# Start order, tails by column half and a norm by columns in a one-core decoder kernel

## The chip, the cores and the metric

The kernel runs on one core of one Trainium2 chip. The metric is the device time of one execution in microseconds, from launch to end, with inputs and outputs in the chip's memory. A core has five engines with queues of their own: TensorE (PE in the profile, with its weight loads PEld), VectorE (DVE), ScalarE (ACT), GpSimd (POOL) and SyncE (SP, which here issues nearly all DMAs). [...]

## The reference, cut to what matters

Input x has 256 positions of 2048 float32 features. Two layers follow each other; every layer is a mixer and then a gated ConvFFN, and both add to x.

```python
def gla_mixer(x, ...):                      # layer 0
    xn = rms_norm(x, norm_w)
    q, k, v, g = split(xn @ w_in)           # 1024, 1024, 2048, 2048 columns
    log_a = log_sigmoid((xn @ gk_w1) @ gk_w2 + gk_b) / 16
    ...                                     # chunked linear attention, 4 heads
    return (rms_norm(o) * silu(g)) @ w_out

def moba_mixer(x, ...):                     # layer 1; 256 positions are one block
    q = rms_norm(rms_norm(x, norm_w) @ w_q) # per head
    k, v = split(rms_norm(x, kv_norm) @ kv_w)
    ...                                     # causal softmax with a relative bias
    return o @ w_out

def conv_ffn(x, norm_w, w_up, conv_w, conv_b, w_down):
    h = rms_norm(x, norm_w) @ w_up          # 2048 -> 2 * 5632
    a, u = split(causal depthwise conv of width 3 over h, plus conv_b)
    return (silu(a) * u) @ w_down           # 5632 -> 2048
```

An rms_norm divides each position by the root of the mean square over its 2048 features and multiplies by a gain for each feature. The kernel multiplies the gain into x before the matrix product and divides by the root only after it.

## The kernel before, in words

Weights are streamed once. `WeightStream` reads them in chunks of 128 x 2048 float32 (1 MB) into three buffers `wraw`, on SP's queue, and hands them out as halves of 1024 columns. A half is split for TensorE into a rounded part `whi` (ACT, line 120) and a remainder `wlo` (DVE, line 121); every product is formed from hi x hi, hi x lo and lo x hi. Three pairs of `whi`/`wlo` buffers rotate, so splitting runs up to two halves ahead of TensorE (`AHEAD`). Fetching a half is a `step()`. Before it fetches, `step()` runs the jobs that are due: `after(n, job)` registers a job for n steps later. That is how norms, transposes and attention are placed between matrix products. The final order of the instructions on each engine is set by the scheduler of the framework when the program is built, from its own estimate of times; dependencies are kept for whole tiles.

The residual lives transposed, feature by position: eight tiles `h[p]` of 256 features x 256 positions, loaded by SP in `load_x` (line 190) between the first weight chunks (`ws.cuts`, `ws.lead`, lines 192 to 205). `make_xw` (lines 213 to 220) forms the gained operand `xw` of one pair p: hi on ACT (line 217), remainder on DVE (line 218). `add_squares` (222) accumulates squares, `token_rstd` (249) sums them over features: `spread_sum` (242) with two matmuls against a matrix of ones gives the root for all 256 positions along the free axis, and with `columns` two more matmuls (line 254) give it as two columns, one position to a partition; `rsqrt` (230) turns the sums into 1/root with Ln and Exp on ACT and one Newton step.

The order of the work:

- Values (`w_v`): `gemm_tok` (289), four groups of 512 columns, each over the eight pairs of x, one step of 12 matmuls a pair; the result has positions on partitions, and `v_out` (356) scales it by the column form of the root.
- Keys, queries, gate and output projection: `gemm` (275).
- FFN up: 44 times `gemm`, two steps each. FFN down: `down` (597), two blocks of 1024 output columns. A block goes over 22 pairs k of hidden features in the order of `ORDERS`; a pair marked "+" is done in seven products of 128 x 128 x 512 in place of eight (Strassen's scheme, which needs sums of weights, lines 94 to 96, on DVE), a plain pair in eight. The eight accumulators are PSUM banks p[1] to p[8]; p[2] and p[3] are the two halves of one tile `low`, p[4] and p[8] tiles of their own. p[2] and p[4] take the first 512 columns (for the two halves of the positions), p[3] and p[8] the other 512. After a block's last seven-product pair `u_sums` (659) combines the Strassen banks; after its last step `sums` adds the four others (line 726 in layer 0, line 705 in layer 1).
- In layer 0 the two blocks come out position by feature and are turned back by `back` (730): four transposes (line 737), an add into `h[q]` (739), then `nrm.feed(q)`, which makes the operand for the next product. The first four run inside block 1, the last four after the following product `w_mq` has begun; `after(5, nrm.close)` ends the norm. `h` has been parked in DRAM meanwhile and is loaded back by POOL (`load_back`).
- In layer 1 the sums are written to the output, 256 KB a time, three by SP and one by ACT (line 707).
- `bias_rows` (775) prepares the relative bias; `head_norm` (794) needs the column form of `n_q`; nothing reads its other form.

Of the kernel before, what the change touches and what calls it, by code (L numbers as in the profile page):

```python
# [8 lines left out]
F32 = mybir.dt.float32  # L9
# [28 lines left out]
def _order(text):  # L38
# [6 lines left out]
           _order("0 2 4 6 8 10 1+ 12 3+ 14 5+ 16 7+ 17 9+ 18 11+ 19 13+ 20 15+ 21")],  # L45
          [_order("0 2 4 1+ 6 3+ 8 5+ 10 7+ 12 16 9+ 14 11+ 17 13+ 18 15+ 19 20 21"),
           _order("0 1+ 2 3+ 4 5+ 6 7+ 8 16 9+ 10 11+ 12 17 13+ 14 15+ 18 19 20 21")]]


class WeightStream:  # L50
# [4 lines left out]
    def __init__(self, nc, raw, parts):  # L55
        self.nc, self.raw, self.parts = nc, raw, parts
# [4 lines left out]
        self.sums, self.slot = {}, None  # L61
# [37 lines left out]
    def prefetch(self, i):  # L99
        nc = self.nc  # L100
        while self.n_split < len(self.halves):
            n = self.n_split
            c, o, kind = self.halves[n]
            if n > i + self.AHEAD + (kind != "plain"):
                break
            self._dma(c + 1)
            for c_, _, kind_ in self.halves[n:n + 3]:
                if kind_ == "b11" and c_ not in self.sums:
                    self._dma(c_ + 1)
                    self._sums(c_)  # L110
            src = self.sums[c][kind] if kind in ("t13", "t24") else self.tiles[c][:, o:o + 1024]
            if kind == "b11":
                src = src[:, :512]
            if kind != "plain" and n % 4 == 3:
                hi, lo = self.slot([128, 1024], F32R, "whi"), self.slot([128, 1024], F32R, "wlo")
            else:
                hi = self.parts.tile([128, 1024], F32R, name="whi")
                lo = self.parts.tile([128, 1024], F32R, name="wlo")
            for a, b in ((0, 512), (512, 1024)) if n == 0 else ((0, src.shape[1]),):
                nc.scalar.copy(hi[:, a:b], src[:, a:b])  # L120
                nc.vector.tensor_sub(lo[:, a:b], src[:, a:b], hi[:, a:b].bitcast(F32))  # L121
# [15 lines left out]
def trunk(ctx: ExitStack, tc: tile.TileContext, xT, cst, msk, w1p, w2a, w_k, w_qa, w_v, w_g, w_go,  # L137
# [23 lines left out]
    ws = WeightStream(nc, raw, parts)  # L161
    plan = [(w_v, 4, 8192), (w_k, 4, 4096), (w_qa, 4, 4096), (w_g, 8, 4096), (w_go, 8, 4096),
# [42 lines left out]
    ws.lead[5, 0] = [load_rest]  # L205
# [4 lines left out]
    def col(c):  # L210
        return cs[:, c:c + 1]

    def make_xw(p, c, name):
        x = slot([128, 2, 2 * S], F32R, name)
        for i in range(2):
            n = col(c + 2 * p + i)
            A.activation(x[:, i, :S], h[p][:, i, :], AF.Copy, scale=n)  # L217
# [4 lines left out]
    def add_squares(p, acc):  # L222
        if p == 0:
            A.activation(acc, h[p], AF.Square)
        else:
            sq = temp("hsq")
            A.activation(sq, h[p], AF.Square)
            V.tensor_add(acc, acc, sq)
# [20 lines left out]
    def token_rstd(acc, columns):  # L249
# [39 lines left out]
    def gemm_tok(xs):  # L289
        ps = acc_ps.tile([128, 2, 512], F32, name="acc")  # L290
        for q0 in range(0, KT, 2):
            hi, lo = step()
            for k in range(2):
                kt = q0 + k
                x = xs(kt)
                wh, wl = hi[:, k * 512:(k + 1) * 512], lo[:, k * 512:(k + 1) * 512]
                for t in range(2):
                    xh, xl = x[:, 128 * t:128 * t + 128], x[:, S + 128 * t:S + 128 * t + 128]
                    T.matmul(ps[:, t, :], xh, wh, start=kt == 0, stop=False)  # L299
                    T.matmul(ps[:, t, :], xh, wl, start=False, stop=False)  # L300
                    T.matmul(ps[:, t, :], xl, wh, start=False, stop=kt == KT - 1)  # L301
        ws.prefetch(cur[0])
        return ps
# [21 lines left out]
    class Norm:  # L325


        def __init__(self, c, name, columns=False):
            self.c, self.name, self.columns, self.xs = c, name, columns, []
# [27 lines left out]
    def v_out(v, ps, n):  # L357

        r0, r1 = (n.rstd[:, S + t:S + t + 1] for t in range(2))
# [237 lines left out]
    def down(layer, hid, ready, jobs):  # L597
# [5 lines left out]
        for b, order in enumerate(ORDERS[layer]):  # L603
# [31 lines left out]
            for i, (k, seven) in enumerate(order):  # L635
# [20 lines left out]
            ws.prefetch(cur[0])  # L656
            sums(b, p)

    def u_sums(p, r):
# [33 lines left out]
    def last_down(hid):  # L693
        def ready(b, p):
# [8 lines left out]
            def end(b, p):  # L703
                for x, n, t, c in zip(r, (2, 3, 4, 8), (0, 0, 1, 1), (0, 1, 0, 1)):
# [13 lines left out]
    def first_down(hid, nrm):  # L718
        blocks = {}

        def ready(b, p):
            blocks[b] = r = u_sums(p, None)

            def end(b, p):
                for x, n in zip(r, (2, 3, 4, 8)):
                    V.tensor_add(x, x, p[n])
# [41 lines left out]
    n_q = Norm(C_MN, "xw", True)  # L768
# [25 lines left out]
    def head_norm(ps, name):  # L794
        t_, sq = slot([128, 2, 512], F32, name), slot([128, 2, 512], F32, "hsq")
        for t in range(2):
            r = n_q.rstd[:, S + t:S + t + 1]
# [73 lines left out]
    after(1, bias_rows)  # L871
# [57 lines left out]

def _quads(w, orders):  # L930
# [4 lines left out]
    q = np.stack([q[g][:, [k for k, _ in order]] for g, order in enumerate(orders)])  # L935
    return _chunks(q.reshape(n // 1024, 128, -1))
# [71 lines left out]
```

## Time and profile before

| | |
|---|---|
| median of 3 runs | 2235.82 us (2235.37 to 2242.01) |
| profiled execution | 2235.57 us |
| its span, first to last instruction | 2233.8 us |
| PE busy | 2212.4 us, 11778 matmuls |
| DVE, ACT, POOL busy | 1659.1, 1263.9, 42.4 us |
| read from HBM | 420.22 MB |

A row of the timeline gives the start and the length in us, then the engine, the line of the kernel, the operation, what it writes and reads, and in brackets how long the engine had been idle and what released it. "x6" merges six like instructions. SPq, ACTq and POOLq are the queues in which DMAs are issued. In the list of waits the numbers are the total in us, the count and the longest. PE's matmuls overlap, so the spacing of their starts and not their length tells the rate.

### The profile page before, as it was taken

How to read it: one execution, taken by the hardware profiler on the slowest of the kernel's cores; microseconds unless marked ns; L12 is line 12 of the kernel's file. 1: busy time of each engine (PE TensorE's matmuls, PEld its weight loads, DVE VectorE, ACT ScalarE, POOL GpSimd, SP SyncE). 2: the span in 40 equal slices, each digit the busy share in tenths (PEclk: the TensorE clock that was granted, in tenths of full speed). 3: DMA queues.
4: the chain of work that ended last, by engine and by line, in shares of the span. 5: the costliest groups of instructions: out<-in, count | busy, mean ns of one | idle time of the engine just before them, and what ended most of it. 6: DMA issues, size and time to landing. Idle time of an engine off the chain costs nothing.

```text
span 2233.8 us, 30207 instructions
## 1 busy us (share of the span) xinstructions
PE 2212.4 (99%) x11778; PEld 1899.6 (85%) x11778; DVE 1659.1 (74%) x2283; ACT 1263.9 (57%) x1759; POOL 42.4 (2%) x59
## 2 busy tenths in 40 slices
PE   7999999999999999999999999999999999999999
PEld 6889888888888888788878888888888888888887
DVE  6566776787777777878866676567777777788886
ACT  6555654655555555545556565456555555555553
POOL 0000000000000000000010000000000000000000
PEclk9999999999999999999999999999999999999999
DMA  6554456555555555565655545456555555556653
GB/s 239 188 188 146 160 198 215 195 189 195 192 191 189 189 189 189 208 222 174 233 202 189 172 168 170 164 192 201 198 189 189 190 189 190 192 194 214 240 202 142
DMA packets 63441, 428.49 MB, mean 192 GB/s; under 512 B 7441, under 2 KB 7969, under 8 KB 13378
## 3 DMA queue, kind: packets, MB, share of 16 engines
q1 hardware_dynamic: 59634, 415.43, 54.1%
q0 software_dynamic: 3232, 10.56, 1.4%
q8 instruction: 92, 1.51, 0.3%
q10 hardware_dynamic: 432, 0.57, 0.1%
q14 instruction: 51, 0.42, 0.1%
HBM read 420.22 MB, written 6.32 MB: 191 GB/s over the span
## 4 chain that ended last, share of the span: by engine, by line
PE 94%; DVE 3%; DMA 2%; issue 1%; ACT 0%; SPq 0%; DVEq 0%; ACTq 0%
PE acc L284 39%; PE acc L285 20%; PE acc L624 10%; PE p L624 6%; PE acc L300 5%; PE acc L301 5%; PE acc L299 5%; DMA wraw<-w_dn 2%; DVE wlo L121 1%; DVE t L94 1%; PE sT L482 0%; ACT whi L120 0%; PE tr L814 0%; DMA wraw<-w_v 0%; PE s L832 0%
## 5 line engine op out<-in xcount | busy, mean ns | idle before, releaser
L121 DVE TENSOR_TENSOR wlo<-wraw,whi 128x1024 fp32r<-128x1024 f32 (+1 forms) x785 | 937.4, 1200 | 441.7 <-ACT whi L120 436.5
L120 ACT CAST whi<-wraw 128x1024 fp32r<-128x1024 f32 (+1 forms) x785 | 807.8, 1034 | 775.1 <-PE acc L284 448.9
L284 PE MATMUL acc<-xw,whi 128*128 128x512 f32 x3328 | 1157.9, 392 | 0.0
L285 PE MATMUL acc<-xw,wlo 128*128 128x256 f32 x3328 | 932.1, 280 | 0.0
L284 PEld LDWEIGHTS acc<-xw,whi 128*128 128x128 f32 x3328 | 622.8, 187 | 137.7
L285 PEld LDWEIGHTS acc<-xw,wlo 128*128 128x128 f32 x3328 | 628.7, 189 | 0.2
L624 PE MATMUL acc<-whi,hid 128*128 128x512 f32 x576 | 204.5, 390 | 0.0
L624 PE MATMUL p<-whi,hid 128*128 128x512 f32 x512 | 180.1, 390 | 0.0
L624 PEld LDWEIGHTS acc<-whi,hid 128*128 128x128 f32 x576 | 108.1, 188 | 22.5 <-ACT whi L120 0.4
L120 ACT CAST whi<-t 128x1024 fp32r<-128x1024 f32 x64 | 67.5, 1054 | 82.6 <-PE p L624 74.5
L624 PE MATMUL acc<-wlo,hid 128*128 128x512 f32 x288 | 112.8, 392 | 0.5 <-DVE wlo L121 0.3
L624 PEld LDWEIGHTS p<-whi,hid 128*128 128x128 f32 x512 | 96.1, 188 | 20.1
L299 PE MATMUL acc<-whi,xw 128*128 128x512 f32 x256 | 100.8, 394 | 12.4 <-ACT xw L217 11.6
L300 PE MATMUL acc<-wlo,xw 128*128 128x512 f32 x256 | 101.2, 395 | 1.0 <-DVE wlo L121 1.0
L301 PE MATMUL acc<-whi,xw 128*128 128x512 f32 x256 | 100.6, 393 | 0.0
L300 PE MATMUL acc<-wlo,xkv 128*128 128x512 f32 x256 | 100.6, 393 | 0.0
L299 PE MATMUL acc<-whi,xkv 128*128 128x512 f32 x256 | 100.5, 393 | 0.0
L301 PE MATMUL acc<-whi,xkv 128*128 128x512 f32 x256 | 100.4, 392 | 0.0
L581 ACT ACTIVATE au<-up,cs 128x256 f32<-128x256 f32 x176 | 95.9, 593 | 7.3 <-DVE up L577 7.3
L624 PE MATMUL p<-wlo,hid 128*128 128x512 f32 x256 | 99.7, 389 | 0.0
L121 DVE TENSOR_TENSOR wlo<-t,whi 128x1024 fp32r<-128x1024 f32 x64 | 77.8, 1221 | 25.8 <-ACT whi L120 25.4
L624 PE MATMUL acc<-whi,comb 128*128 128x512 f32 x256 | 89.9, 389 | 0.0
(254 smaller groups left out, 2356.6 us busy)
## 6 DMA issues: line engine op xcount, KB each, us to landing
wraw<-w_up SPq DMA_DIRECT2D x176, 1024.0 KB, 4.8
wraw<-w_dn SPq DMA_DIRECT2D x88, 1024.0 KB, 4.9
wraw<-w_g SPq DMA_DIRECT2D x16, 1024.0 KB, 4.8
wraw<-w_go SPq DMA_DIRECT2D x16, 1024.0 KB, 4.9
wraw<-w_mq SPq DMA_DIRECT2D x16, 1024.0 KB, 4.8
wraw<-w_kk SPq DMA_DIRECT2D x16, 1024.0 KB, 4.8
wraw<-w_kv SPq DMA_DIRECT2D x16, 1024.0 KB, 4.8
wraw<-w_mo SPq DMA_DIRECT2D x16, 1024.0 KB, 4.8
```

Source lines behind the costliest of these rows:

```text
L94: V.tensor_sub(t13, src[:, 512:1536], src[:, 0:1024])
L120: nc.scalar.copy(hi[:, a:b], src[:, a:b])
L121: nc.vector.tensor_sub(lo[:, a:b], src[:, a:b], hi[:, a:b].bitcast(F32))
L284: T.matmul(ps[:, b, :], hi[:, c:c + 128], x, start=kt == 0, stop=False)
L285: T.matmul(ps[:, b, :S], lo[:, c:c + 128], x[:, :S], start=False, stop=kt == kts - 1)
L299: T.matmul(ps[:, t, :], xh, wh, start=kt == 0, stop=False)
L300: T.matmul(ps[:, t, :], xh, wl, start=False, stop=False)
L301: T.matmul(ps[:, t, :], xl, wh, start=False, stop=kt == KT - 1)
L581: A.activation(au[:, i, :], t[:, i, :], AF.Identity, bias=col(cb + n), scale=col(cw + 2 * 2 * FT + n))
L624: T.matmul(p[n], xp, wp, start=n not in begun, stop=left[n] == 0)
```

## The change

Four things are done.

1. Start. The first two column groups of the values are stored side by side (`w_v2`) and computed together: `gemm_tok(xs, 2)` takes for each pair of x two steps, one for each group, in two accumulators. x is therefore needed half as often during the first 16 steps. Loads on SP are cut and ordered anew: 512 columns of weights, the two halves of x pair 0, 512 columns, 1024 columns, x pair 1, then whole chunks of 1 MB with one pair of x after each. The first norm's 16 gain columns get a tile of their own, `gn`, loaded first on ACT's queue, ahead of the rest of `cs` and of the activation table. `issue_after` puts the second half of the first weight split and the first squares behind the first operand on ACT.
2. Tails. Of each block of `down`, up to three plain pairs at the end (two in block 1 of layer 0, three in the others) are done first for the one half of the columns (p[2], p[4]) and then for the other (p[3], p[8]); `sums` runs once after each half. The weights are stored in that order. One entry of `ORDERS` changes, so that block 1 of layer 0 has two plain pairs at its end and five in place of six at its beginning.
3. After block 1 of layer 0. Turning back begins earlier: pairs 0 and 1 at index 2 of block 1, pair 4 inside its tail, pairs 5, 6 and 7 one, two and three steps into the next product; the norm closes after 4 steps. Parked tiles are loaded back at indices 0 and 1. `bias_rows` moves from 1 step to 12 steps into that product.
4. One norm by columns. `n_q` skips `spread_sum` and `rsqrt`; `column_rstd` makes two matmuls, a small DVE operation and a power on POOL.

The diff, without the plain consequences in names and arguments:

```diff
@@ -42,23 +42,28 @@
 ORDERS = [[_order("0 2 4 1+ 6 3+ 8 5+ 10 7+ 12 16 9+ 14 11+ 17 13+ 18 15+ 19 20 21"),
-           _order("0 2 4 6 8 10 1+ 12 3+ 14 5+ 16 7+ 17 9+ 18 11+ 19 13+ 20 15+ 21")],
+           _order("0 2 4 6 8 1+ 10 3+ 12 5+ 14 7+ 16 9+ 17 11+ 18 13+ 19 15+ 20 21")],
...
+def _tail(order):
+    return min(3, len(order) - 1 - max(i for i, (_, seven) in enumerate(order) if seven))
@@ -117,7 +122,8 @@
             for a, b in ((0, 512), (512, 1024)) if n == 0 else ((0, src.shape[1]),):
-                nc.scalar.copy(hi[:, a:b], src[:, a:b])
+                with self.tc.issue_after(self.first) if a else nullcontext():
+                    nc.scalar.copy(hi[:, a:b], src[:, a:b])
@@ -158,8 +164,8 @@
-    plan = [(w_v, 4, 8192), (w_k, 4, 4096), (w_qa, 4, 4096), (w_g, 8, 4096), (w_go, 8, 4096),
+    plan = [(w_v2, 1, 16384), (w_v, 2, 8192), (w_k, 4, 4096), (w_qa, 4, 4096), (w_g, 8, 4096), (w_go, 8, 4096),
@@ -181,17 +187,19 @@
     V.memset(one, 1.0)
+    gn = keep.tile([128, KT], F32, name="gn")
+    A.dma_start(gn, cst[:, C_GN:C_GN + KT])
+    A.dma_start(cs[:, :C_CW], cst[:, :C_CW])
...
     V.memset(mhalf, -0.5)
-    A.dma_start(cs[:, :C_CW], cst[:, :C_CW])
...
-    ws.cuts = {0: ((0, 512), (512, 1024), (1024, 1536), (1536, 2048)), 1: ((0, 1024), (1024, 2048))}
-    for p, at in ((0, (0, 0)), (1, (0, 512)), (2, (0, 1024)), (3, (1, 0)), (4, (1, 1024)), (5, (2, 0)), (6, (2, 0)),
-                  (7, (3, 0))):
+    ws.cuts = {0: ((0, 512), (512, 1024), (1024, 2048))}
+    for p, at in ((0, (0, 0)), (1, (0, 1024)), (2, (1, 0)), (3, (2, 0)), (4, (3, 0)), (5, (4, 0)), (6, (5, 0)),
+                  (7, (6, 0))):
@@ -202,26 +210,28 @@
-    ws.lead[5, 0] = [load_rest]
+    ws.lead[7, 0] = [load_rest]
...
     def col(c):
-        return cs[:, c:c + 1]
+        return gn[:, c - C_GN:c - C_GN + 1] if C_GN <= c < C_GN + KT else cs[:, c:c + 1]
...
             n = col(c + 2 * p + i)
-            A.activation(x[:, i, :S], h[p][:, i, :], AF.Copy, scale=n)
+            hi = A.activation(x[:, i, :S], h[p][:, i, :], AF.Copy, scale=n)
+            ws.first = ws.first or hi.ins
...
         if p == 0:
-            A.activation(acc, h[p], AF.Square)
+            with tc.issue_after(ws.first):
+                A.activation(acc, h[p], AF.Square)
@@ -250,11 +260,24 @@
         spread_sum(ps[:, :S], acc[:, 0])
-        for t in range(2 if columns else 0):
-            T.matmul(ps[:, S + t:S + t + 1], acc[:, 0, 128 * t:128 * t + 128], one, start=True, stop=True)
         n = S + 2 if columns else S
+        if columns:
+            sum_columns(ps[:, S:], acc)
...
         rsqrt(r[:, :n], ps[:, :n], 1.0 / D, (128, n))
+        return r[:, :S], r[:, S:]
+    def sum_columns(ps, acc):
+        for t in range(2):
+            T.matmul(ps[:, t:t + 1], acc[:, 0, 128 * t:128 * t + 128], one, start=True, stop=True)
+    def column_rstd(acc):
+        ps = bank("sum_h", (128, 2))
+        V.tensor_add(acc[:, 0], acc[:, 0], acc[:, 1])
+        sum_columns(ps, acc)
+        m, r = (small.tile([128, 2], F32, name=n) for n in ("mean_h", "col_h"))
+        V.tensor_scalar(m, ps, 1.0 / D, EPS, op0=OP.mult, op1=OP.add)
+        nc.gpsimd.tensor_tensor(r, m, mhalf[:, :2], op=OP.pow)
@@ -286,21 +309,22 @@
-    def gemm_tok(xs):
-        ps = acc_ps.tile([128, 2, 512], F32, name="acc")
+    def gemm_tok(xs, groups=1):
+        out_ = [acc_ps.tile([128, 2, 512], F32, name="acc") for _ in range(groups)]
         for q0 in range(0, KT, 2):
+            for ps in out_:
+                hi, lo = step()
+                for k in range(2):
+                    kt = q0 + k
...
         ws.prefetch(cur[0])
-        return ps
+        return out_ if groups > 1 else out_[0]
@@ -337,14 +361,17 @@
         def close(self):
-            self.rstd = token_rstd(self.acc, self.columns)
-    nrm = Norm(C_GN, "xw", True)
+            if self.rows:
+                self.rstd, self.col = token_rstd(self.acc, self.columns)
+            else:
+                self.col = column_rstd(self.acc)
+    nrm = Norm(C_GN, "xw", columns=True)
...
     for p in range(2, NP):
-        after(p - 1, lambda p=p: nrm.operand(p))
+        after(2 * p - 3, lambda p=p: nrm.operand(p))
@@ -428,9 +455,11 @@
     after(26, gate_decay)
-    for hd in range(GH):
+    for hd, ps in enumerate(gemm_tok(xs, 2)):
+        after(2 * hd + 1, lambda hd=hd, ps=ps: v_out(vg[hd], ps, nrm))
+    for hd in (2, 3):
         ps = gemm_tok(xs)
-        after((10, 3, 0, 0)[hd], lambda hd=hd, ps=ps: v_out(vg[hd], ps, nrm))
+        after(0, lambda hd=hd, ps=ps: v_out(vg[hd], ps, nrm))
@@ -632,7 +661,8 @@
             last = max(i for i, (k, seven) in enumerate(order) if seven)
-            for i, (k, seven) in enumerate(order):
+            tail = [k for k, _ in order[len(order) - _tail(order):]]
+            for i, (k, seven) in enumerate(order[:len(order) - len(tail)]):
@@ -653,8 +683,17 @@
                     sums = ready(b, p)
-            ws.prefetch(cur[0])
-            sums(b, p)
+            for f, (n0, n1) in enumerate(((2, 4), (3, 8))):
+                for i, k in enumerate(tail):
+                    for job in todo.get((f, i), ()):
+                        job()
+                    w = step()
+                    todo_ = [(n, t, a) for a in range(2) for n, t in ((n0, 0), (n1, 1))]
+                    for n, t, a in sorted(todo_, key=lambda x: x[1]) if i == len(tail) - 1 else todo_:
+                        prod(n, part(k, a, t), w, a)
+                if f:
+                    ws.prefetch(cur[0])
+                sums(f, (n0, n1))
@@ -672,11 +711,11 @@
         V.tensor_add(u3, u2, p[7])
+        V.tensor_add(r[2], r[2], u3)
         V.tensor_add(u2, u2, p[5])
+        V.tensor_add(u3, u3, p[5])
         V.tensor_add(r[1], r[1], u2)
-        V.tensor_add(r[2], r[2], u3)
         V.tensor_add(r[3], r[3], u3)
-        V.tensor_add(r[3], r[3], p[5])
@@ -700,8 +739,9 @@
-            def end(b, p):
-                for x, n, t, c in zip(r, (2, 3, 4, 8), (0, 0, 1, 1), (0, 1, 0, 1)):
+            def end(c, ns):
+                for t, n in enumerate(ns):
+                    x = r[2 * t + c]
@@ -753,19 +793,21 @@
-        jobs = {3 + q: [lambda q=q: back(q, in_acc)] for q in range(4)}
-        for m, i in enumerate((1, 2, 15, 16)):
+        jobs = {2: [lambda q=q: back(q, in_acc) for q in (0, 1)]}
+        for q, i in ((2, 3), (3, 4), (4, (1, 1))):
+            jobs.setdefault(i, []).append(lambda q=q: back(q, in_acc))
+        for m, i in enumerate((0, 1, 15, 16)):
...
         down(0, hid, ready, {1: jobs})
-        for q in range(4, NP):
-            after(1 + (q - 4) // 2, lambda q=q: back(q, lambda: bank("hf", (128, 2, S))))
-        after(5, nrm.close)
+        for q in (5, 6, 7):
+            after(q - 4, lambda q=q: back(q, lambda: bank("hf", (128, 2, S))))
+        after(4, nrm.close)
...
         after(6 + 2 * p, lambda p=p: park(p))
-    n_q = Norm(C_MN, "xw", True)
+    n_q = Norm(C_MN, "xw", rows=False, columns=True)
@@ -868,7 +910,7 @@
     xkv = []
-    after(1, bias_rows)
+    after(12, bias_rows)
```

`_both_groups` stores, for each 256 rows, the 1024 columns of group 0 and then those of group 1; `_quads` stores a block's tail by column halves.

More of the change, by code (lines that the diff above doesn't have):

```diff
@@ L1 @@
 import math
-from contextlib import ExitStack
+from contextlib import ExitStack, nullcontext
 import concourse.bass as bass
@@ L60, in __init__ @@
         self.cuts, self.lead = {}, {}
-        self.sums, self.slot = {}, None
+        self.sums, self.slot, self.first = {}, None, None
     def add(self, w, g, cols):
@@ L136, in trunk @@
 @with_exitstack
-def trunk(ctx: ExitStack, tc: tile.TileContext, xT, cst, msk, w1p, w2a, w_k, w_qa, w_v, w_g, w_go,
+def trunk(ctx: ExitStack, tc: tile.TileContext, xT, cst, msk, w1p, w2a, w_k, w_qa, w_v2, w_v, w_g, w_go,
           w_up0, w_dn0, w_kk, w_kv, w_mq, w_mo, w_up1, w_dn1, rel, onehot, out):
@@ L287, in gemm @@
         return ps
-    def gemm_tok(xs):
-        ps = acc_ps.tile([128, 2, 512], F32, name="acc")
+    def gemm_tok(xs, groups=1):
+        out_ = [acc_ps.tile([128, 2, 512], F32, name="acc") for _ in range(groups)]
         for q0 in range(0, KT, 2):
[L292 to L301, printed above, removed]
+            for ps in out_:
+                hi, lo = step()
+                for k in range(2):
+                    kt = q0 + k
+                    x = xs(kt)
+                    wh, wl = hi[:, k * 512:(k + 1) * 512], lo[:, k * 512:(k + 1) * 512]
+                    for t in range(2):
+                        xh, xl = x[:, 128 * t:128 * t + 128], x[:, S + 128 * t:S + 128 * t + 128]
+                        T.matmul(ps[:, t, :], xh, wh, start=kt == 0, stop=False)
+                        T.matmul(ps[:, t, :], xh, wl, start=False, stop=False)
+                        T.matmul(ps[:, t, :], xl, wh, start=False, stop=kt == KT - 1)
         ws.prefetch(cur[0])
-        return ps
+        return out_ if groups > 1 else out_[0]
     def rows(xs):
@@ L325, in trunk, with __init__ @@
     class Norm:
[L328 to L329 removed]
+        def __init__(self, c, name, rows=True, columns=False):
+            self.c, self.name, self.rows, self.columns, self.xs = c, name, rows, columns, []
             self.acc = keep.tile([128, 2, S], F32, name="acc_sq", tag="acc_sq")
@@ L357, in v_out @@
     def v_out(v, ps, n):
-        r0, r1 = (n.rstd[:, S + t:S + t + 1] for t in range(2))
+        r0, r1 = (n.col[:, t:t + 1] for t in range(2))
         A.activation(v[0][:, 0, :], ps[:, 0, :], AF.Copy, scale=r0)
@@ L722, in ready, with end @@
             blocks[b] = r = u_sums(p, None)
-            def end(b, p):
-                for x, n in zip(r, (2, 3, 4, 8)):
-                    V.tensor_add(x, x, p[n])
+            def end(c, ns):
+                for t, n in enumerate(ns):
+                    V.tensor_add(r[2 * t + c], r[2 * t + c], p[n])
             return end
@@ L934, in _quads @@
     q = np.stack([q[..., 0, 0, :], q[..., 0, 1, :], q[..., 1, 1, :], q[..., 1, 0, :]], axis=3)
-    q = np.stack([q[g][:, [k for k, _ in order]] for g, order in enumerate(orders)])
-    return _chunks(q.reshape(n // 1024, 128, -1))
+    rows_ = []
+    for g, order in enumerate(orders):
+        n_tail = _tail(order)
+        body, tail = (q[g][:, [k for k, _ in part]] for part in (order[:-n_tail], order[-n_tail:]))
+        tail = tail[:, :, [0, 3, 1, 2]].reshape(128, n_tail, 2, 2, 512).transpose(0, 2, 1, 3, 4)
+        rows_.append(np.concatenate([body.reshape(128, -1), tail.reshape(128, -1)], axis=1))
+    return _chunks(np.stack(rows_))
 def _pairs(w):
```

14 lines of the change are left out of this document (9 added, 5 removed).

## The prediction

> **What bounds the kernel now.** First the page's totals and its chain, then the waits of TensorE's weight loads (they stand ahead of the matmuls, so a stall shows there in full), then the timeline at the places that the change touches.
>
> ```profile
> span 2233.8 us, 30207 instructions
> PE 2212.4 (99%) x11778; PEld 1899.6 (85%) x11778; DVE 1659.1 (74%) x2283; ACT 1263.9 (57%) x1759; POOL 42.4 (2%) x59
> PE 94%; DVE 3%; DMA 2%; issue 1%; ACT 0%; SPq 0%; DVEq 0%; ACTq 0%
> ...
> PEld acc L299 <- ACT xw L217: 11.6, 1, 11.6
> PEld acc L624 <- DVE wlo L121: 8.8, 14, 1.6
> ...
> 999.21 5.44 PE acc L624 x24
> ```
>
> TensorE bounds it: 99% busy, 94% of the chain. 24 matmuls in a row take 5.44 us, 0.227 us apiece, and their number hardly changes. What can be won is the 21.4 us in which PE does nothing (2233.8 - 2212.4): 11.6 us in one wait at the start, waits for splits in the down products, a few us behind the last matmul. The sum is made against the profiled execution's 2235.57 us, 1.8 us over its span and 0.25 us under the median of 2235.82.
>
> **Start.** The rows of ACT, DVE and PE, then the DMA rate in half microseconds from 0 to 20 us:
>
> ```profile
> 1.19 0.89 SPq L190 DMA_DIRECT2D h<-xT  x2
> 3.85 0.62 ACT L120 CAST whi<-wraw 128x512 fp32r<-128x512 f32 x1 [1.83 <-DMA wraw<-w_v]
> 4.05 0.16 DVE L772 SCALAR_TENSOR_TENSOR kqw<-cs 128x1 f32<-128x1 f32 x1 [3.03 <-DMA cs<-cst]
> 4.50 0.69 DVE L121 TENSOR_TENSOR wlo<-wraw,whi 128x512 fp32r<-128x512 f32 x1 [0.28 <-ACT whi L120]
> 4.71 0.63 ACT L224 ACTIVATE acc_sq<-h 128x512 f32<-128x512 f32 x1 [0.25 <-DMA h<-xT]
> 6.40 0.62 ACT L120 CAST whi<-wraw 128x512 fp32r<-128x512 f32 x1 [1.06 <-DMA wraw<-w_v]
> 8.05 0.63 ACT L227 ACTIVATE hsq<-h 128x512 f32<-128x512 f32 x1 [1.03 <-DMA h<-xT]
> 9.49 0.63 ACT L227 ACTIVATE hsq<-h 128x512 f32<-128x512 f32 x1 [0.81 <-DMA h<-xT]
> 10.14 1.05 ACT L120 CAST whi<-wraw 128x1024 fp32r<-128x1024 f32 x1
> 11.09 2.50 ACT L217 ACTIVATE xw<-h,cs 128x256 fp32r<-128x256 f32 x6
> 11.22 1.23 DVE L121 TENSOR_TENSOR wlo<-wraw,whi 128x1024 fp32r<-128x1024 f32 x1 [0.37 <-ACT whi L120]
> 11.65 0.79 PE L299 MATMUL acc<-whi,xw 128*128 128x512 f32 x1 [11.65 <-ACT xw L217]
> 14.34 0.63 PE L301 MATMUL acc<-whi,xw 128*128 128x512 f32 x1
> 14.77 0.63 PE L299 MATMUL acc<-whi,xw 128*128 128x512 f32 x1
> 16.22 0.40 PE L300 MATMUL acc<-wlo,xw 128*128 128x512 f32 x1
> 22.15 0.39 PE L299 MATMUL acc<-whi,xw 128*128 128x512 f32 x1
> ...
> GB/s 0 0 0 53 181 250 345 336 234 176 205 225 274 266 307 385 365 397 356 344 328 426 414 438 389 508 393 426 446 385 369 397 391 399 386 384 409 459 383 492
> ```
>
> x pair 0, the gains and the first weights are there at 4.71 us, but `xw` stands on ACT behind the second cast, three squares, which wait for their own loads, and a third cast. The 37th matmul, that is the end of three steps, comes at 22.15.
>
> After: `gn` is issued first and can be there by 4.05, where the whole `cs` was. ACT casts the first 512 columns (3.85 to 4.47), then makes `xw` in pieces of 0.42 us (2.50 / 6) from about 4.5. First matmul: about 5.0. From there data set the pace. The second 512 columns are the fourth load as before (6.40). The next are 1024 columns as one load: 1.25 MB queued up to there, between the fifth load before (1.0 MB, 8.05) and the sixth (1.5 MB, 9.49), say 8.8; cast to 9.85, `wlo` (1.23) to 11.1. Step 0, at 0.43 us a matmul (14.34 to 14.77), is over by about 10, step 1 waits for that `wlo` and ends at 11.1 + 11 x 0.227 = 13.6. Step 2 needs chunk 1, now one load of 1 MB, 2.5 MB queued (2.62 million bytes). By 9.5 us the rate row adds up to 2.18 million bytes moved while 1.57 had landed, a lag of 0.61; 2.62 + 0.61 = 3.23 are moved at 12.2. Cast to 13.25, `wlo` to 14.5: step 2's second matmul starts there, and three steps are done at 14.5 + 2.5 = 17.0, against 22.15: **-5.2 us**. Afterwards x is asked for every 5.4 us and weights every 2.7 us per half, 1.25 MB in 5.44 us or 240 GB/s, below the nearly 400 that the row shows, so nothing is given back. Ends: no lag at all, 2.62 million moved at 10.7, and step 1's end at 13.6 binds, 13.6 + 2.7 = 16.3: -5.8; or chunk 1 at the slowest rate after the sixth load (205 GB/s, 5.1 us after 9.49), at 14.6: -2.8. I take the value from the lag, which the same queue showed.
>
> [...]
>
> On SP, whole chunks stand ahead of pairs 2 to 7 of x, needed only at steps 4, 6 and so on. `load_rest` comes two chunks later; its users run from step 12 (`gate_split`), 25 us later than that: nothing. `v_out` of group 0 and 1 moves to steps 17 and 19; the third accumulator carries group 2, group 3 needs the first at step 24: nothing, with five steps of cover.
>
> **Behind block 1 of layer 0.** The waits from 1115 to 1150 us and their rows, with the rows of the norm:
>
> ```profile
> PEld acc L300 <- DVE wlo L121: 1.1, 1, 1.1
> PEld acc L299 <- ACT whi L120: 1.0, 1, 1.0
> ...
> 1135.92 1.04 ACT L120 CAST whi<-wraw 128x1024 fp32r<-128x1024 f32 x1 [1.47 <-PE acc L301]
> 1136.99 1.23 DVE L121 TENSOR_TENSOR wlo<-wraw,whi 128x1024 fp32r<-128x1024 f32 x1
> ...
> 1140.91 0.28 PE L247 MATMUL sum_h<-sum_parts,ones 128*128 128x256 f32 x1
> 1141.03 0.40 PE L299 MATMUL acc<-whi,xw 128*128 128x512 f32 x1
> ...
> 1150.98 1.67 POOL L804 TENSOR_TENSOR rr<-ss,mhalf 128x8 f32<-128x8 f32 x1 [7.52 <-DVE ss L802]
> ```
>
> Pairs 6 and 7 come back so late that a split is made only after PE has run dry. With pairs 4 to 7 turned at the tail and in steps 0 to 2 in place of 1 and 2 twice over, each has a step of slack: **-2.1**; the other end is 0, should DVE be as late as now. A pair costs DVE some 3.2 us with its split, a step lasts 2.7, so the lag grows by half a microsecond a pair and stays below one step. The two `spread_sum` matmuls go at 0.12 us each (1140.91 to 1141.03): **-0.2**. `rsqrt` (DVE, ACT, two table loads) is off the path; the power on POOL costs 1.67 us as in L804 and is used 8 steps in: nothing. `bias_rows` goes to step 12, its two matmuls cost the same there, and POOL's DMAs behind it serve the softmax only: nothing.
>
> **Inside block 1 of layer 0.** The waits from 1000 to 1115 us:
>
> ```profile
> PEld acc L624 <- DVE wlo L121: 1.9, 3, 0.7
> PEld acc L624 <- ACT whi L120: 0.4, 1, 0.4
> ```
>
> 2.3 us are lost where turning back meets the first seven-product pairs. Now it is over one index before the first of them, but that pair comes one plain pair (5.4 us) earlier. I take a third, **-0.8**; ends -2.3 and, should the earlier pair miss its weight sums, +1.5, about as much again as two of the waits above.
>
> **Tails.** The matmuls are the same. New is that p[3] shares its tile with p[2]: its first matmul of the tail waits for the DVE add of p[2]. Queued behind it is all of PE. In front of it stand the matmuls of p[8], in a bank of their own: 18 x 0.227 = 4.1 us in three tails, 2.7 us in the short one; the add takes 0.64. Nothing, bounds 0 and +1.5 in all. In layer 1, two outputs of block 0 stand on SP in front of weight loads about 8 us earlier than before, with three buffers full: nothing.
>
> **End.**
>
> ```profile
> 2227.73 1.28 DVE L705 TENSOR_TENSOR res<-res,acc 128x512 f32<-128x512 f32 x2 [9.93 <-PE acc L624]
> 2228.66 0.39 PE L624 MATMUL p<-whi,hid 128*128 128x512 f32 x1
> 2228.93 1.28 DVE L705 TENSOR_TENSOR res<-res,p 128x512 f32<-128x512 f32 x2
> 2230.24 0.34 ACTq L707 DMA_DIRECT2D out_dram<-res  x1
> ...
> out_dram<-res SPq DMA_DIRECT2D x3, 256.0 KB, 2.1
> out_dram<-res ACTq DMA_DIRECT2D x1, 256.0 KB, 2.3
> ```
>
> Four adds and four outputs follow the last matmuls. Two of each move 8 us up. The last two adds still follow each other, since p[3] ends with p[8]: the last ends 1.5 us after the last matmul's start, as now (2228.66 to 2230.21). The last output no longer queues behind three: 2.0 in place of 2.3, **-0.3** (ends 0 and -0.8).
>
> Sum: -5.2 - 2.1 - 0.2 - 0.8 - 0.3 = -8.6; 2235.57 - 8.6 = **2227.0 us**, 0.4% under the median. About 0.3% (6.7 us, 2229.1) is what a measurement of this kernel can tell from no change.
>
> **Rivals.** (1) The start gains little: chunk 1, now in one piece, lands late. For: from 4 to 6 us the rate is 176 to 250 GB/s. Against: later it is near 400. With -2.8 in place of -5.2: 2229.4. (2) The wait inside block 1 grows, +1.5 in place of -0.8: 2229.3. Seven-product pairs are DVE's heaviest stretch; but turning back no longer overlaps them. [...] (4) The other side: PE waits for the add of p[2] in the tails. DVE runs strictly in order and the add stands behind splits that wait for buffers and loads. It decides from 15.3 us lost in all (8.6 to give back and 6.7), 3.8 us a tail over the cover of 4.1: 2242.5 or more. Against it: before, too, the adds stood behind splits and no such wait is in the list. (5) The first operand is as late as before because `gn` lands late: without the -5.2, 2232.2.
>
> **How the numbers follow.** Forecast 0.60; (1) 0.13; (2) 0.08; (3) 0.08; (4) 0.07; (5) 0.04. The forecast and (3) are faster, 0.68, (1), (2) and (5) within 0.3%, 0.25, (4) slower, 0.07. The range reaches from 2224.0 (start -5.8, block 1 -2.3, end -0.8, the rest as forecast: 2224.4) to 2232.5, which takes in all but (4) and the combinations of misses; the faster cases alone would be 2224 to 2229.
>
> **What would show it.** First matmul near 5 us; the 37th near 17 in place of 22.15. No wait over 0.5 us from the end of block 1 of layer 0 on for 35 us; fewer than 2.3 us of waits inside it. No wait for DVE's add in any tail. Two outputs in flight at the end. A later first matmul, waits for `res` or `c` adds, or new waits in the 20 us after the start would prove it wrong.

## The result and the profile after

The changed kernel is slower: 2246.64 us (2243.88 to 2248.24) against 2237.44 us (2235.37 to 2242.01) for the kernel before in the same eight rounds, a ratio of 1.0037, 95% interval [1.0027, 1.0048]. The forecast was 2227.0 us with a range up to 2232.5. The profiled execution took 2244.39 us, 8.8 us more than the one of before.

The totals on the page of the changed kernel:

```profile
span 2242.6 us, 30203 instructions
PE 2226.1 (99%) x11776; PEld 1901.9 (85%) x11776; DVE 1659.1 (74%) x2279; ACT 1260.5 (56%) x1754; POOL 44.1 (2%) x60
```

The waits of its TensorE's weight loads over the whole span (total in us, count, longest):

```profile
PEld acc L653 <- DVE wlo L127: 12.8, 19, 1.6
PEld acc L323 <- ACT xw L225: 5.0, 1, 5.0
PEld acc L324 <- DVE wlo L127: 2.2, 3, 1.0
PEld acc L653 <- ACT whi L126: 1.5, 3, 0.5
PEld tr L856 <- issue: 0.6, 1, 0.6
```

The idle time of PE fell, from 21.4 us to 16.5 (2242.6 - 2226.1). But its busy time rose by 13.7 us, from 2212.4 to 2226.1, with two matmuls fewer. So neither a longer wait nor another engine explains the loss: the same matmuls took longer.

Where, shows a count of matmuls in equal stretches. The view by windows gives for each stretch PE's busy time, in brackets the number of matmuls, the granted clock, the DMA share and GB/s. Of before:

```profile
110.00:170.00 60.00, 60.00 (x341) 1.00 0.54 184
260.00:320.00 60.00, 60.00 (x348) 1.00 0.59 205
500.00:600.00 100.00, 100.00 (x579) 1.00 0.56 190
1600.00:1700.00 100.00, 100.00 (x579) 1.00 0.56 190
```

The same view of the changed kernel:

```profile
260.00:320.00 60.00, 60.00 (x342) 1.00 0.58 199
500.00:600.00 100.00, 100.00 (x567) 1.00 0.55 189
1600.00:1700.00 100.00, 100.00 (x579) 1.00 0.56 190
```

In each of these stretches PE does nothing but the pairs of `gemm` (512 columns, then 256) and is busy throughout at a granted clock of 1.00. Yet from 500 to 600 us it does 567 matmuls where before did 579; from 1600 to 1700 us it does 579 in both. And before itself had both rates: 341 in 60 us from 110, 348 in 60 us from 260. The timeline of the changed kernel at 500 us shows the slow one:

```profile
500.02 0.28 PE L308 MATMUL acc<-xw,wlo 128*128 128x256 f32 x1
500.13 0.40 PE L307 MATMUL acc<-xw,whi 128*128 128x512 f32 x1
500.37 0.28 PE L308 MATMUL acc<-xw,wlo 128*128 128x256 f32 x1
500.49 0.40 PE L307 MATMUL acc<-xw,whi 128*128 128x512 f32 x1
500.73 0.28 PE L308 MATMUL acc<-xw,wlo 128*128 128x256 f32 x1
500.85 0.40 PE L307 MATMUL acc<-xw,whi 128*128 128x512 f32 x1
501.08 0.28 PE L308 MATMUL acc<-xw,wlo 128*128 128x256 f32 x1
```

To the nanosecond the starts follow each other by 233, 117, 241, 120, 236, 113: 1060 ns for three pairs, 353.3 a pair. In the fast rhythm they follow by 230 and 117, 346.7 a pair. The difference is 1.9%. By the spacing of three pairs, the long slow stretches are: in before 107 to 173 us; in after 102 to 167 and, without a break but for the norm's two matmuls, 242 to 889 us, where before is fast (248 to 882).

Start of one matmul against the same matmul of before: at the first -6.7 us, at the 37th -5.5, at 240 us -5.7, at 888 us +6.4. That is 12.1 us lost in the slow stretch. From there to the first matmul of layer 1's down products 0.9 us are lost, in these products 1.7; behind the last matmul 0.2 are won: +8.8 in all.

### The profile page after: what moved, and what is told of

Read it like the earlier page. It is cut to its first block, busy times and chain, and to the rows that moved or that the text cites. A ratio compares the mean times of both kernels' runs of the same rounds, so it can differ in the third digit from the quotient of the medians.

```text
span 2242.6 us, 30203 instructions
## 1 busy us (share of the span) xinstructions
PE 2226.1 (99%) x11776; PEld 1901.9 (85%) x11776; DVE 1659.1 (74%) x2279; ACT 1260.5 (56%) x1754; POOL 44.1 (2%) x60
## 4 chain that ended last, share of the span: by engine, by line
PE 91%; DVE 4%; DMA 3%; issue 1%; ACT 1%; DVEq 0%; ACTq 0%
PE acc L307 40%; PE acc L308 20%; PE acc L653 8%; PE p L653 5%; PE acc L324 5%; PE acc L325 5%; PE acc L323 5%; DMA wraw<-w_dn 3%; DVE wlo L127 2%; ACT whi L126 1%; DVE t L99 1%; PE sT L511 0%; DMA wraw<-w_v 0%; PE tr L856 0%; PE s L874 0%
## 5 line engine op out<-in xcount | busy, mean ns | idle before, releaser
L307 PE MATMUL acc<-go,whi 128*128 128x512 f32 x256 | 90.5, 399 | 0.0
```

The costliest lines, as they stand in the source:

```text
L307: T.matmul(ps[:, b, :], hi[:, c:c + 128], x, start=kt == 0, stop=False)
```

## The experiments

Theory 1: TensorE has two rhythms for these pairs, is left in one or the other by the small matmuls between them, and keeps it; no operand, transfer or engine of the change makes the stretch slow. Theory 2: something that the change moves does, its tiles or its loads. Beside that, the smaller terms were taken apart. The new lines compute nothing that is used.

### A short insert between two pairs (after_idle, before_idle)

```diff
+    def idle_turn():
+        tp = bank("idle", (128, 512))
+        for i in range(4):
+            T.transpose(tp[:, 128 * i:128 * i + 128], h[i // 2][:, i % 2, :128], ident)
+    after(12, idle_turn)
     go = []
```

> The changed kernel with four transposes more, whose result nobody reads, on TensorE at about 255 us, inside the first long stretch of gemm. Theory 1 (rhythm): from about 242 to 888 us TensorE runs the pairs of gemm in a slower one of two rhythms (353.3 ns a pair in place of 346.7), and nothing in the work decides which; a short insert of transposes switches it. Then the pairs go at 346.7 ns from 255 us to 888 us, 630 us x 1.9% = 12 us are won, less 0.5 us for the transposes: about 2235. Theory 2 (the change itself, by its moved tiles or its other order of loads, makes each matmul of the stretch slower): the spacing stays at 353.3 ns and the time is about 2247.1.

> The kernel before with the same four transposes at the same place (about 261 us in its time). Theory 1 (rhythm): the pairs, at 346.7 ns from 248 us on, go at 353.3 ns from there to 882 us, 12 us are lost: about 2249.5. Theory 2 (only the change's tiles or loads bring the slow rhythm): no change but 0.5 us, about 2237.9.

The changed kernel so: 2246.12 us, ratio to before 1.0044 [1.0027, 1.0061]; the insert, at 244.8 us, did not switch it (568 matmuls from 500 to 600 us). The kernel before so: 2239.33 us, 1.0011 [1.0001, 1.0020]: it was switched from fast to slow, 738 matmuls from 260 to 390 us in place of 752, until the norm's two small matmuls at 410 us switched it back. The two rows, of before and of before with the insert:

```profile
260.00:390.00 130.00, 130.00 (x752) 1.00 0.60 209
260.00:390.00 130.00, 130.00 (x738) 1.00 0.60 204
```

That the slow rhythm comes without any part of the change speaks against theory 2, but that an insert switches it every time was wrong.

### The start alone, and all but the start (start_only, no_start)

The two kernels differ from before and after by the whole of the change's first part; of its diff:

```diff
-    for hd in range(GH):
-        ps = gemm_tok(xs)
-        after((10, 3, 0, 0)[hd], lambda hd=hd, ps=ps: v_out(vg[hd], ps, nrm))
+    for hd, ps in enumerate(gemm_tok(xs, 2)):
+        after(2 * hd + 1, lambda hd=hd, ps=ps: v_out(vg[hd], ps, nrm))
...
```

> The kernel before with the new start alone (side-by-side values, loads, gains tile). Both theories: first matmul near 5 us and 5.5 us ahead of before until 170 us. Theory 1: the rhythm from 242 us on is what TensorE happens to leave the attention inserts in; the program up to there is that of the changed kernel, so the slow one is likeliest: 2237.4 - 5.7 + 12.1 = about 2243.8. If the other parts of the change bring the slow rhythm: about 2231.7.

> The changed kernel with the start of before. Theory 1: the program up to 880 us is that of before, so 346.7 ns a pair from 248 us on; what is left is the rest of the change as the two traces show it: inside block 1 of layer 0 +3.4, behind it -3.1, from there to layer 1's down products +1.0, in them +1.7: 2237.4 + 3.0 = about 2240.4. If the slow rhythm comes with the tails, the norm or the turning back: about 2252.

The start alone: 2242.22 us, 1.0023 [1.0014, 1.0033], slow from 241 to 888 us. All but the start: 2239.12 us, 1.0011 [1.0002, 1.0021], fast from 409 to 885 us. So the slow stretch comes with the start. How, can be followed to the nanosecond. When the second sums of the third attention head come in (222.8 us in after, 228.6 in before), both kernels are in the fast rhythm; the matmul ahead of them is spaced 236 to 237 ns in the three traces with the old start and 233 to 234 in the three with the new; the 22 small matmuls that follow are the same; then the old goes on in the slow rhythm and the new in the fast one. The next insert turns both round. Within each group the traces agree within 2 ns. So a shift of 3 ns in the phase at which an insert meets PE goes with 12 us. In both kernels these 22 matmuls stand in the middle of a pair, between its matmul of 512 columns and its one of 256; in before:

```profile
228.33 0.40 PE L284 MATMUL acc<-xw,whi 128*128 128x512 f32 x1
228.57 0.28 PE L247 MATMUL sum_o<-sum_parts,ones 128*128 128x256 f32 x1
...
230.95 0.36 PE L285 MATMUL acc<-xw,wlo 128*128 128x256 f32 x1
```

One thing stays open: the profiled run of the kernel without the new start turned slow by itself at 264 us, between two pairs, until 407 us. It was also its slowest run (2242.45 us). Only one execution of each kernel was traced; before itself had executions of up to 2246.09 us beside medians of about 2236 to 2238, and whether the rhythm turned in them is not shown.

### An insert in the middle of a pair (after_pin, start_pin)

```diff
                 T.matmul(ps[:, b, :], hi[:, c:c + 128], x, start=kt == 0, stop=False)
+                if idle and cur[0] > idle[0]:
+                    idle.pop(0)
+                    tp = bank("idle", (128, 512))
+                    for i in range(4):
+                        T.transpose(tp[:, 128 * i:128 * i + 128], hs[0][:, 0, i % 2, :128], ident)
...
+    idle.append(cur[0] + 12)
     go = []
...
+    idle.append(cur[0] + 5)
     for p in range(NP):
         after(6 + 2 * p, lambda p=p: park(p))
```

> The changed kernel with four idle transposes at about 252 us and four at about 412 us, now put between the two matmuls of a pair, where the traces so far show that such an insert is followed by the fast rhythm from either state (203, 239, 117, 235 ns and then 230 and 117); between two pairs it was followed by the slow one here. Theory 1 (a rhythm that TensorE is left in): 346.7 ns a pair from there to 888 us, 625 us x 1.9% = 11.7 us won, less 1 us for the inserts: about 2236. Theory 2 (the operands or transfers of this stretch make it slow): 353.3 ns again after each insert, about 2247.6.

2234.06 us (2232.43 to 2235.25), 0.9991 [0.9981, 1.0000]: 12.6 us under the changed kernel by the medians, 10 by the two ratios. The timeline of this kernel at the first insert:

```profile
244.14 0.40 PE L309 MATMUL acc<-xw,whi 128*128 128x512 f32 x1
244.38 0.28 PE L315 MATMUL acc<-xw,wlo 128*128 128x256 f32 x1
244.49 0.40 PE L309 MATMUL acc<-xw,whi 128*128 128x512 f32 x1
244.72 0.60 PE L314 MATMUL idle<-mk,h 128*128 128x128 f32 x4
245.08 0.36 PE L315 MATMUL acc<-xw,wlo 128*128 128x256 f32 x1
245.28 0.40 PE L309 MATMUL acc<-xw,whi 128*128 128x512 f32 x1
...
246.33 0.39 PE L309 MATMUL acc<-xw,whi 128*128 128x512 f32 x1
246.56 0.28 PE L315 MATMUL acc<-xw,wlo 128*128 128x256 f32 x1
246.68 0.39 PE L309 MATMUL acc<-xw,whi 128*128 128x512 f32 x1
246.91 0.28 PE L315 MATMUL acc<-xw,wlo 128*128 128x256 f32 x1
```

Its matmuls in two stretches, by windows:

```profile
260.00:390.00 130.00, 130.00 (x752) 1.00 0.60 208
500.00:600.00 100.00, 100.00 (x579) 1.00 0.56 190
```

Ahead of the insert the starts follow each other in the slow rhythm, behind it by 230 and 117 ns, with the same operands, buffers and loads. The counts show that it lasts: 752 and 579 matmuls, where the changed kernel has 738 and 567. In between, the norm's two small matmuls at 399 us turned it slow, and the second insert, at 403.6 us, turned it back. This decides for theory 1 and prices it: the 12 us of the sum.

The place in the pair is not enough, though. Four transposes there were followed by the fast rhythm in every trace of alternating pairs, whichever came before: the kernels' own at 1558 to 1574 us (ten times from the slow one, five from the fast) and the idle ones put there, two in each of four kernels. Other small matmuls in the middle of a pair were not: the 22 of before at 228.6 us, above, and the norm's at 399 us here were followed by the slow one.

> The kernel before with the new start alone and the two idle inserts in the middle of a pair. Theory 1: the start by itself wins its 5.7 us and the rhythm was the whole of what start_only lost: 2242.2 - 12 + 1 = about 2231. If a start's gain is given back elsewhere: 2236 or more.

The start alone with the same two inserts: 2230.53 us, 0.9971 [0.9959, 0.9983]. Its span is 2228.4 us against 2233.8 of before, -5.4: the start keeps what it wins.

### Another order, and a shift of no work (order, after_shift, before_shift)

```diff
-                T.matmul(ps[:, b, :S], lo[:, c:c + 128], x[:, :S], start=False, stop=kt == kts - 1)
+                todo_.append((ps[:, b, :S], lo[:, c:c + 128], x[:, :S], kt == kts - 1))
+                if len(todo_) == 2:
+                    for o_, l_, x_, last in todo_:
+                        T.matmul(o_, l_, x_, start=False, stop=last)
+                    todo_ = []
```

> The changed kernel with two 512-column matmuls and then two 256-column ones in place of alternating ones, all through gemm. Theory 1: the slow rhythm needs the alternation and its 767 us in the changed kernel go at the fast rate, -14 us, about 2232.5. If the slow rhythm belongs to the operands or transfers: no gain, about 2246.6; if a weight load behind a short matmul is the limit, slower than that.

2238.87 us, 1.0012 [1.0002, 1.0021]: 7.8 us under the changed kernel by the medians, 5.6 by the ratios. Its windows:

```profile
500.00:600.00 100.00, 100.00 (x576) 1.00 0.56 190
1600.00:1700.00 100.00, 100.00 (x576) 1.00 0.55 189
```

Two long and then two short matmuls go at about 348 ns a pair in every long stretch: one rhythm, nearly the fast one. The 346.7 expected was a little too good, and 9.5 us of splits were waited for inside block 1 of layer 0, where after has 5.7.

```diff
-    for lag, job in ((2, gla_scores), (4, gla_values), (6, gla_norm)):
+    for lag, job in ((2, gla_scores), (4, gla_values), (7, gla_norm)):
```

> The changed kernel with the second sums of the attention heads one step later, which moves two small matmuls a head and no work. Theory 1: from 242 us on either rhythm can come out: 2246.6 or 12 us less. Theory 2 (operands, transfers): slow rhythm and 2246.6.

> The kernel before with the same shift. Theory 1: either rhythm can come out from 248 us on, 2236.5 or up to 12 us more. Theory 2: fast rhythm, 2236.5.

2246.69 us (1.0041 [1.0026, 1.0056]) and 2237.04 us (0.9995 [0.9985, 1.0005]): neither turned in the long stretch, which fits both theories. In the stretches ahead of it both did: the changed kernel so is slow from 206 to 212 us and from 222 on, where it was fast from 206 to 212 and from 226 to 231, and before so is slow from 213 to 219, where it was fast from 212 to 218. So where two small matmuls stand can turn the rhythm for some microseconds, in kernels with the same start.

### Tails, turning back, bias rows (no_tail, no_turn, bias_only)

The changed kernel with the old `down` and `end`, and with the old order of pairs and jobs (which leaves block 1 of layer 0 a tail of one pair); of the second:

```diff
-           _order("0 2 4 6 8 1+ 10 3+ 12 5+ 14 7+ 16 9+ 17 11+ 18 13+ 19 15+ 20 21")],
+           _order("0 2 4 6 8 10 1+ 12 3+ 14 5+ 16 7+ 17 9+ 18 11+ 19 13+ 20 15+ 21")],
...
-        jobs = {2: [lambda q=q: back(q, in_acc) for q in (0, 1)]}
+        jobs = {3 + q: [lambda q=q: back(q, in_acc)] for q in range(4)}
```

> The changed kernel without the tails (down products, sums and outputs as before; pairs 4 to 7 turned back 1 to 4 steps into the next product, the norm closing after 5). The slow rhythm stays (the program up to 880 us is the same), so 2246.6 less what the tails cost. If the tails cost the 1.7 us that layer 1's down products lost, and part of the 3.4 us inside block 1 of layer 0: about 2243.5, with waits for splits of 4.6 us in layer 1's down products in place of 6.3. If they cost nothing: 2246.6 and some 6.3 us of waits there.

> The changed kernel with the order of pairs and the turning back of before, in and behind block 1 of layer 0. Slow rhythm as in the changed kernel. If the earlier turning back and the earlier seven-product pair cost the 3.4 us inside block 1 and brought the 3.1 us behind it: waits inside the block fall from 5.7 to about 2.3 us, those behind it come back (about 3 us), and the time stays near 2246.6. If the tail of block 1 costs it: 5.7 us of waits stay.

Without the tails 2245.21 us (1.0041 [1.0027, 1.0056]), which the times don't tell from the changed kernel; with the old turning back 2243.19 us (1.0032 [1.0020, 1.0044]). The waits inside block 1 of layer 0 in the changed kernel:

```profile
PEld acc L653 <- DVE wlo L127: 4.2, 7, 1.6
PEld acc L653 <- ACT whi L126: 1.5, 3, 0.5
```

The same with the old turning back:

```profile
PEld acc L653 <- DVE wlo L127: 2.1, 3, 1.0
PEld acc L653 <- ACT whi L126: 0.5, 1, 0.5
```

The earlier turning back with the earlier seven-product pair costs the 3.1 us between 5.7 and 2.6. It is not the tail: without the tails, but with the new order of pairs, the two are 4.5 and 1.2, again 5.7. (In `no_start` and `order`, which have the new order of pairs too, they come to 8.2 and 9.5; why so much was not tried.) And the waits behind the block did not come back with the old turning back, against what was expected. What had stayed moved there was the bias rows. In before their two matmuls stand ahead of the transposes of pair 6, as its timeline shows:

```profile
1131.65 0.81 PE L781 MATMUL biasrow<-oh,rl 32*16 32x384 f32 x2
1132.39 0.65 PE L737 MATMUL hf<-mk,c 128*128 128x128 f32 x4
```

> The kernel before with bias_rows 12 steps into the product behind block 1 of layer 0 in place of 1, nothing else. If the bias rows, whose matmul and bank stand ahead of the turning back of pair 6, cause the 2.7 us of waits behind that block: these waits go, 0.6 us come back at the later place, and the time falls by about 2 us, to 2235. If it is the steps at which pairs 4 to 7 are turned back, as the prediction had it: the waits stay and the time is that of before.

```diff
-    after(1, bias_rows)
+    after(12, bias_rows)
```

2235.74 us, 0.9992 [0.9980, 1.0004]. Its trace has no wait of a weight load in the 40 us behind the block, where before has 2.7 us, and one new wait later in its list:

```profile
PEld tr L837 <- issue: 0.6, 1, 0.6
```

So this line alone takes the waits away; the time does not tell its 2 us from nothing. Pair 6 is turned back at 1128.74 us here in place of 1132.39; that it had waited for the bias rows' bank is likely and not shown. (In this trace layer 1's down products took 1.2 us more than in before.)

The tails in layer 1: from the first to the last matmul of its down products, seven traces with tails took 232.5 to 234.1 us (mean 233.3), nine without 230.7 to 233.1 (mean 231.7). They cost about 1.6 us by the means, though the ranges overlap; the changed kernel and the same without tails differ by 1.1 (233.6 and 232.5). The waits of weight loads there, in the changed kernel:

```profile
PEld acc L653 <- DVE wlo L127: 6.3, 9, 1.3
```

And without tails:

```profile
PEld acc L653 <- DVE wlo L127: 5.1, 8, 1.4
```

None is for an add of DVE. In the changed kernel, DVE's first weight sum of block 1 waits 2.40 us for its load:

```profile
2129.03 1.23 DVE L99 TENSOR_TENSOR t<-wraw 128x1024 f32<-128x1024 f32 x1 [2.40 <-DMA wraw<-w_dn]
```

In before it does not wait:

```profile
2119.86 1.22 DVE L94 TENSOR_TENSOR t<-wraw 128x1024 f32<-128x1024 f32 x1
```

Which is that load and what held it wasn't tried.

### The best of it (best, best12)

New start, norm by columns, old order and turning back, two inserts in the middle of a pair; first with the bias rows at 1 step, then at 12. Tails were meant to stay in layer 0:

```diff
 def _tail(order):
+    if order in ORDERS[1]:
+        return 0
     return min(3, len(order) - 1 - max(i for i, (_, seven) in enumerate(order) if seven))
...
```

> New start, norm by columns, tails by column half in layer 0 alone (three pairs in block 0, one in block 1), order and turning back of before, bias rows where they were, two idle inserts in the middle of a pair. Theory: after_pin's 2234.1, less the 2.6 us that no_turn won between the start of block 1 of layer 0 and layer 1's down products, less 1.7 us of the tails of layer 1 and 0.6 us of the bias rows: about 2229.5. If the tails or the turning back cost nothing by themselves: 2234.

> The kernel best with the bias rows at 12 steps. If the bias rows cause the waits behind block 1 of layer 0: 2230.7 - 2.0 = about 2228.7. If not: 2231.

The test compares orders by their content, and block 0 of layer 0 has the same order as block 0 of layer 1. So block 0 of layer 0 lost its tail too, against what was expected, and only the tail of one pair in block 1 of layer 0 is left. That the tails cost nothing in layer 0 these two kernels can't show.

2230.70 us (0.9969 [0.9957, 0.9980]), with the 2.7 us of waits behind the block back; and 2228.27 us (2227.47 to 2228.81), 0.9959 [0.9944, 0.9974], with none of them: faster than both kernels, by 0.4% of before. The totals on its page:

```profile
span 2225.7 us, 30215 instructions
PE 2212.1 (99%) x11784; PEld 1901.9 (85%) x11784; DVE 1656.7 (74%) x2279; ACT 1260.9 (57%) x1754; POOL 44.1 (2%) x60
```

PE's busy time is that of before again (2212.1 and 2212.4), its idle time 13.6 us in place of 21.4.

## Why the prediction was wrong

- **What bounds the kernel** is the part that failed: "24 matmuls in a row take 5.44 us, 0.227 us apiece, and their number hardly changes. What can be won is the 21.4 us in which PE does nothing". That took PE's busy time as fixed; it rose by 13.7 us. It held two rates of `gemm`, and the change, by moving the start, turned 640 us from one to the other: +12.1 us, a term that the sum does not have and for which there was no rival. The time came out where rival 4 had put it, but none of that rival's waits is in the trace. The two window rows of before above (341 and 348 matmuls in 60 us) were there to be read.
- **Start**, -5.2: right. First matmul 4.97 us (said: about 5.0), the 37th at 16.69 (17.0), so -5.5; `start_pin` holds it to the end (-5.4 in span). Rivals 1 and 5 fell. The sum let step 0 go at 0.43 us a matmul and step 1 at 0.227; no run shows what ends the slower rate. In the changed kernel it ended at about 9.7 us, with step 0's last matmul and 4.7 us after its first (in before at about 15.8, 4.1 after the first), and PE still waited for a split after that, 0.63 us up to 14.06. Two readings of the rate row were off without harm to the sum: from 4 to 6 us it has 176 to 234 GB/s, not 250, and the 205 of the bound -2.8 stands at 5 us, while behind 9.49 us its lowest is 328. Two rows of the changed kernel's timeline:

```profile
4.97 0.80 PE L323 MATMUL acc<-whi,xw 128*128 128x512 f32 x1 [4.97 <-ACT xw L225]
...
16.69 0.62 PE L323 MATMUL acc<-whi,xw 128*128 128x512 f32 x2
```

- **Behind block 1 of layer 0**, -2.1: all 2.7 us of waits went and 0.6 us came up in front of `tr`, so the sum is right, but by luck. The bias rows, priced at "nothing", bring the gain by themselves (`bias_only`), and with them moved the old turning back has no waits either (`no_turn`). What the new turning back would do with the bias rows in their old place was not run.
- **Inside block 1**, -0.8 with ends -2.3 and +1.5: the waits grew from 2.3 to 5.7 us, +3.4, outside both ends. Turning back over "one index before the first" seven-product pair did not clear it; `no_turn` shows 2.6. Rival 2 named the mechanism and put it at less than half its price.
- **Tails**, nothing with ends 0 and +1.5: about +1.6, all in layer 1. Right in that PE never waits for the add of p[2] (rival 4). That DVE's order can hold ready work back is shown elsewhere: in before a split whose `whi` was there at 1017.66 us stood behind a weight sum that waited 1.90 us for its load, and started at 1019.23. What the tails cost stands in the waits for splits, and why is open. **End**, -0.3: from the start of the last matmul to the end 4.97 us in place of 5.14, -0.2. **spread_sum**, -0.2: two matmuls less, as said.

Without the rhythm the steps come to -3.3 us (8.8 - 12.1) in place of -8.6; `after_pin`, at 2234.06 with its two inserts, would have missed the range too.

## What to carry to other kernels

When an engine is 99% busy, count its instructions in equal stretches of the same work before taking its busy time as fixed; two counts for one loop, here 567 and 579 matmuls in 100 us, are a term of the sum, and here a change far away, in the start, switched it. This loop of long and short matmuls was pinned by four transposes in the middle of a pair (2234.06 us) or by putting two long and two short together (2238.87), where the changed kernel took 2246.64; other inserts did not do it, so each is to be counted again in a trace. And take a change of several parts apart on the chip: here the part priced at nothing took the waits behind the block away, and the one that was given that gain cost 3 us inside it.

## What the hardware showed that was not expected

The pairs of 512 and 256 columns have a fast rhythm (230 and 117 ns, 346.7 a pair) and a slow one that repeats after three pairs (353.3 a pair), at a granted clock of 1.00 and without a wait. Either lasts for hundreds of microseconds, the fast one from 248 to 882 us in before, the slow one from 242 to 889 in after. The kernels with the old start and with the new entered one insert some 3 ns apart (236 to 237 ns against 233 to 234) and left it in different rhythms, the same one in each group of three traces. From 500 to 600 us the six traces of alternating pairs with the new start and no idle insert in the middle of a pair were slow, the five with the old start fast. Four transposes in the middle of a pair were followed by the fast rhythm each time (15 times at 1558 to 1574 us, twice in each of four kernels with the idle ones), other small matmuls there by either. Grouped by two the matmuls have one rhythm, about 348 ns. What keeps a rhythm, and what turned it at 264 us without any insert, no run shows.
